# Weight differences of the seven-product pairs on GpSimd, and three more such pairs in the down projection

## The chip, the cores and the metric

The kernel runs on one core of a Trainium2 chip. The metric is the device time of one execution in microseconds (us). Three runs of the kernel before took 1316.18 to 1316.69 us, with a median of 1316.56 us.

A core has five engines that run their own instruction streams in order and wait for each other by semaphores. TensorE (PE in the profile) multiplies matrices and writes to PSUM. VectorE (DVE), ScalarE (ACT) and GpSimd (POOL) work elementwise. SyncE (SP) only issues the weight loads here. The profile lists PE's weight loads as PEld.

## The reference: what is computed

One layer of an encoder trunk on 256 positions with 2048 channels, everything in float32:

```python
h = rms_norm(x, norm_mix)
proj = h @ w_in                          # 2048 -> 9216: u, v | q, k, v | two gates
y_a = gmlp_branch(u, v, ...)             # gelu, layer norm, mixing over 128-position chunks
y_b = neighbourhood_attn(q, k, v, rpb)   # 16 heads, windows on a 4 x 64 grid
merged = sigmoid(g_a) * (y_a @ w_branch_a) + sigmoid(g_b) * (y_b @ w_branch_b)
x = x + merged @ w_out                   # 2048 -> 2048
h = rms_norm(x, norm_ffn)
up = conv3(h @ w_up)                     # 2048 -> 11008, width-3 conv over positions
x = x + (silu(gate) * val) @ w_down      # 5504 -> 2048
return rms_norm(x, norm_final)
```

Almost all of the work is in the weight matrices: w_in, w_branch, w_out, w_up and w_down.

## The kernel before, in words

**Pieces.** All weights are read as a single list of *pieces*, planned before the kernel starts: two row blocks of 128 by 512 columns, or two column blocks of 512 for one row block of 128 (a `plan_wide` piece). `load_to` issues the loads on SP into tiles `wraw`, of which there are `LOAD_AHEAD` (5). `split_to` splits each piece into a high part `whi` (ScalarE copies to float32r, line 151) and a low part `wlo` (VectorE subtracts the high part from the raw weights, line 152); there are four of each, and a piece is split up to three pieces ahead of its use. Activations are split in the same way, and a product is three matmuls: high by high, low activation by high weight, high activation by low weight. In the profile lines 291 to 293 are these three (`triple`).

**Order.** The order of every engine's instructions is the program's own order (`manual_schedule`). `begin(i)` opens piece i: it issues loads, issues the splits of the piece three ahead and then runs the tasks registered for it with `at(i, f)`. So a task at `i - 3` stands, on each engine, three pieces before the products of piece i.

**Wide groups and pairs.** A *wide* group multiplies 256 positions (two blocks t of 128) by 1024 columns (two blocks c of 512). The early projections of v and of the attention values, the second half of the two gates, the output projection (two groups) and the down projection (two groups of 43 pieces) are wide. A plain piece of a wide group is four products, one for each t and c: 12 matmuls. For some *pairs* of pieces, listed in `V_QUADS`, `VA_QUADS`, `GATE_QUADS`, `OUT_QUADS` and `DOWN_QUADS`, the group uses a scheme with seven block products for eight: the first piece of the pair takes three products, the second four. Entry q of such a list stands for the pieces 2q and 2q + 1 of its group.

**What a pair needs.** Sums of activation blocks (`act_sums`, `act_sums_split`, two to five pieces ahead, or made once for several groups) and differences of raw weight blocks:

- `weight_sums` at `i - 3` takes the two raw pieces (kept in `whole`) and makes four differences of 128x512 in two tiles `t13` and `t24`, each by one VectorE subtraction (lines 316 to 319).
- `weight_sums_split` at `i - 2` splits the two tiles into high and low parts `h13`, `l13`, `h24`, `l24`: two ScalarE copies (line 326) and two VectorE subtractions of 128x1024 (line 327).
- the first piece of a pair then needs only its first column block split, the second piece both (`units`).

The tiles of a pair exist once and take the memory of tiles that are idle at that stage (`first_room`, `sums_room`, `down_room`), so the profile shows them by those names: h, t, y, l. There are 29 pairs before: 2 and 3 in the early projections, 3 and 3 in the gates, 2 and 2 in the output projection, 7 and 7 in the down projection.

**GpSimd.** It has little to do: loads of the attention values and of the relative bias (lines 656 and 708), the selects that mask the bias (line 726), the residual x (line 927) and the last gain (line 1272). Its DMAs use descriptors that lie in a reserved part of SBUF.

Of the kernel before, what the change touches and what calls it, by code (L numbers as in the profile page):

```python
# [8 lines left out]
F32 = mybir.dt.float32  # L9
F32R = mybir.dt.float32r  # L10
AF = mybir.ActivationFunctionType
# [25 lines left out]
RMS_EPS = 1e-6  # L37
LN_EPS = 1e-5

LOAD_AHEAD = 5  # L40
SPLIT_AHEAD = 3
WAKE = (9, 8)
V_QUADS, V_ORDER = ((5, 6), (0, 1, 6, 7, 8, 9, 10, 11, 12, 13, 2, 3, 4, 5, 14, 15))
# [12 lines left out]
OUT_ORDER = (tuple(range(16)), (0, 1, 6, 7, 2, 3, 10, 11, 4, 5, 8, 9, 12, 13, 14, 15))  # L56
TURN_X2 = (13, 1)
Y_GAP = 224
DOWN_QUADS = ((4, 6, 9, 11, 14, 16, 18), (3, 5, 8, 10, 13, 15, 17))


@with_exitstack
def trunk_kernel(ctx, tc, x, norm_mix, w_in, ln_g, ln_b, w_s, b_s, rpb, w_branch, w_out,
                 norm_ffn, w_up, conv_k, conv_b, w_down, norm_final, out):
    nc = tc.nc
# [34 lines left out]
    def plan_wide(src, row0, order, c0):  # L100
        first = len(pieces)
        for k in order:
            pieces.append((src, row0 + k * 128, 2, (c0, 512, 1, 0), 512))
        return first
# [7 lines left out]
    def load_to(n):  # L112
        while n_loaded[0] < min(n, len(pieces)):
            i = n_loaded[0]
            n_loaded[0] += 1
            if i in preload:
                for f in preload[i]:
                    f()
            src, r0, kn, (c0, cn, nb, cs), step = pieces[i]
            w = wpool.tile([128, 2, 512], F32, name="wraw", bufs=LOAD_AHEAD)  # L120
            ld = src.shape[-1]
            if i == 0:
                for k in range(kn):
                    nc.sync.dma_start(w[:, k, :cn], src[r0:r0 + 128, c0 + k * step:c0 + k * step + cn])
            elif nb == 1:
                nc.sync.dma_start(
                    w[:, :kn, :cn],
                    bass.AP(tensor=src.tensor, offset=src.offset + r0 * ld + c0,
                            ap=[[ld, 128], [step, kn], [1, cn]]))
            else:  # L130
                for b in range(nb):
                    nc.sync.dma_start(
                        w[:, :kn, b * cn:(b + 1) * cn],
                        bass.AP(tensor=src.tensor, offset=src.offset + r0 * ld + c0 + b * cs,
                                ap=[[ld, 128], [step, kn], [1, cn]]))
            raw[i] = w
            if i in whole:
                whole[i] = w
# [30 lines left out]
    def at(i, f):  # L169
        tasks.setdefault(i, []).append(f)  # L170
# [6 lines left out]
    def begin(i):  # L177
        cur[0] = i
        load_to(i + LOAD_AHEAD)
        if i == 0:  # L180
# [83 lines left out]

    def wide(src, row0, order, c0, acts, quads, room, done, sums=None, odd=None):
        n0 = plan_wide(src, row0, order, c0)
        boxes = {}
        for n, q in enumerate(quads):  # L270
            i = n0 + 2 * q
            own = odd if odd and n % 2 else room
            whole[i] = whole[i + 1] = None
            units[i], units[i + 1] = 1, 2
            b = boxes[q] = {}
            if sums is None:
                b["acts"] = {}
                sum_acts_at(i - 5, i - 4, b["acts"], lambda k=order[2 * q]: ff["ap"][k // 2], room, "s")
            else:
                b["acts"] = sums[order[2 * q]]  # L280
            at(i - 3, lambda i=i, b=b: weight_sums(i, b, room))
            at(i - 2, lambda b=b, own=own: weight_sums_split(b, own))
        return ("wide", n0, order, acts, quads, boxes, done)

    def sum_acts_at(i, j, box, pair, room, name):
        at(i, lambda: act_sums(pair(), box, room))
        at(j, lambda: act_sums_split(box, room, name))
# [25 lines left out]
    def weight_sums(i, box, room):  # L313
        r0, r1 = whole.pop(i), whole.pop(i + 1)
        t13, t24 = room("t13", F32), room("t24", F32)
        nc.vector.tensor_sub(t13[:, 0], r0[:, 1], r0[:, 0])
        nc.vector.tensor_sub(t24[:, 0], r1[:, 1], t13[:, 0])
        nc.vector.tensor_sub(t13[:, 1], r1[:, 1], r0[:, 1])
        nc.vector.tensor_sub(t24[:, 1], r1[:, 0], t24[:, 0])
        box["w"] = (t13, t24)  # L320

    def weight_sums_split(box, room):
        u = []
        for name, t in zip(("13", "24"), box.pop("w")):
            h, l = room("h" + name, F32R), room("l" + name, F32R)
            nc.scalar.activation(h, t, AF.Copy)
            nc.vector.tensor_sub(l, t, h.bitcast(F32))
            u.append((h, l))
        box["t"] = {1: [x[:, 0] for x in u[0]], 3: [x[:, 1] for x in u[0]],
                    2: [x[:, 0] for x in u[1]], 4: [x[:, 1] for x in u[1]]}  # L330

    def run_wide(g, tail=0):
        kind, n0, order, acts, quads, boxes, done = g
# [176 lines left out]
    def first_room(name, dt):  # L510
        return ypool.tile([128, 2, 512], dt, name=f"y{first_rooms.index('t13' if name == 'f' else name)}")
# [387 lines left out]
    def ev_sums(j, room):  # L899
        def done(P, i):  # L900
            x2 = rs["x2"]
            p1, p5, p6, p7 = P
            x11, x12, x21, x22 = (x2[:, t, c * 512:(c + 1) * 512] for t in range(2) for c in (j, j + 1))
            m = {}

            def first_half():
                ab, cd = room("t13", F32), room("t24", F32)
                m["v"], m["u3"], m["w"] = cd[:, 0], cd[:, 1], ab[:, 0]
                nc.scalar.activation(ab[:, 0], p1, AF.Copy)
                nc.vector.tensor_add(x11, p1, x11)  # L910
                nc.vector.tensor_add(ab[:, 1], p6, ab[:, 0])
                nc.vector.tensor_add(m["v"], p5, ab[:, 1])
                nc.vector.tensor_add(m["u3"], p7, ab[:, 1])
                nc.vector.tensor_add(m["w"], p5, m["u3"])

            def second_half():
                nc.vector.tensor_add(x12, x12, m["v"])
                nc.vector.tensor_add(x21, x21, m["u3"])
                nc.vector.tensor_add(x22, x22, m["w"])

            at(i + 1, first_half)
            at(i + 2, second_half)
        return done
# [7 lines left out]
    def ev_out(g):  # L931
        def done(ps, i):
            x2 = rs["x2"]
            for t in range(NT):
                for c in range(2):
                    v = x2[:, t, (2 * g + c) * 512:(2 * g + c + 1) * 512]
                    nc.vector.tensor_add(v, ps[t][c], v)

            def squares(j):
                for t in range(NT):  # L940
                    nc.scalar.activation(junk, x2[:, t, j * 512:(j + 1) * 512], AF.Square,
                                         accum_out=rs["ss"][:, t, j:j + 1])

            for c in range(2):
                at(i + TURN_X2[g] + c, lambda j=2 * g + c: turn_x2(j))
                at(i + 3 + c, lambda j=2 * g + c: squares(j))
            if g == 1:
                at(i + 5, norm2)
        return done
# [7 lines left out]
    def turn_x2(j):  # L957
        x2 = rs["x2"]
        for k2 in range(2):
            p = bank()  # L960
            for kk in range(2):
                c = j * 4 + k2 * 2 + kk
                for t in range(NT):
                    nc.tensor.transpose(p[:, kk * T + t * 128:kk * T + (t + 1) * 128],
                                        x2[:, t, c * 128:(c + 1) * 128], ident)
            k = j * 4 + k2 * 2
            rs["h", k], rs["h", k + 1] = new_pair(hpool, f"h{k // 2}")
            split_pair(p, (rs["h", k], rs["h", k + 1]), gffn[:, k:k + 2])
# [128 lines left out]
    def odd_room(name, dt):  # L1097
        return s_room["odd"].tile([128, 2, 512], dt, name=name)

    first_sums = {2 * q: {} for q, _, _ in X_SUMS}  # L1100
    g_v = wide(w_in2, 0, V_ORDER, V0, xt, V_QUADS, first_room, (ev_v_sums, ev_v), first_sums,
               odd_room)
    g_va = wide(w_in2, 0, VA_ORDER, VA0, xt, VA_QUADS, first_room, (ev_va_sums, ev_va), first_sums)
    for n, (q, i, j) in enumerate(X_SUMS):
        sum_acts_at(i, j, first_sums[2 * q], lambda q=q: x_pairs[q],
                    lambda name, dt, i=i: first_room("s2" if name == "f" and i < 9 else name, dt), f"s{n}")
# [7 lines left out]
    def g_branch(br, j):  # L1114
# [5 lines left out]
    x_sums, m_sums = ({2 * q: {} for q in qs} for qs in (GATE_PAIRS, OUT_PAIRS))  # L1120
# [1 line left out]
                 (ev_gate_sums(br), ev_gate_wide(br)), x_sums) for br in range(2)]  # L1122
    g_m2 = [g_branch(br, j) for j in (2, 3) for br in range(2)]
    g_o = [wide(w_o, 0, OUT_ORDER[g], g * 1024, lambda k: mg["mT"][k], OUT_QUADS[g], sums_room,
                (ev_sums(2 * g, sums_room), ev_out(g)), m_sums) for g in range(2)]
    for n, q in enumerate(GATE_PAIRS):
        i = g_gw[0][1] - 3 + 3 * n
        sum_acts_at(i, i + 1, x_sums[2 * q], lambda q=q: x_pairs[q], sums_room, f"s{n}")
    for n, q in enumerate(OUT_PAIRS):
        i = g_o[0][1] + 3 + 3 * n  # L1130
# [7 lines left out]
    def down_room(name, dt):  # L1138
        return hpool.tile([128, 2, 512], dt, name=h_room[name])

    g_dn = [wide(w_d, 0, range(NF), g * 1024, lambda k: ff["a"][k], DOWN_QUADS[g], down_room,
                 (ev_sums(2 * g, down_room), ev_down if g == 0 else finish)) for g in range(2)]
# [166 lines left out]
```

## Time and profile before

| | before |
|---|---|
| runs (3), median | 1316.56 us |
| the profiled execution: span, first to last instruction | 1314.9 us |
| TensorE busy | 1303.3 us (99%), 6776 matmuls |
| VectorE busy | 1066.2 us (81%) |
| ScalarE busy | 764.8 us (58%) |
| GpSimd busy | 88.3 us (7%) |
| DMA, mean rate | 197 GB/s |
| granted TensorE clock, mean | 0.998 |

The span covers the first to the last instruction; the device time of a run holds a little more than it. A row of the profile's timeline gives the start and the length in us, the engine, the line, the operation, the tiles (out<-in), the shape, and the number of instructions put together; in square brackets stands the idle time of the engine just before, and what ended it. A row of the windows gives a stretch, its length, the busy time of PE, PEld, DVE, ACT and POOL, each with its instruction count, the granted clock, the DMA share and the rate. A row of the waits gives the waiting engine and line, what it waited for, the total, the count and the longest. A row for one line gives shortest/median/longest in ns.

### The profile page before, as it was taken

What the parts mean: (1) busy time and instruction counts of PE and PEld (TensorE: products, weight loads), DVE (VectorE), ACT (ScalarE), POOL (GpSimd) and SP (SyncE); (2) the same over time, 40 slices, a digit from 0 to 9 for tenths busy, and PEclk for the clock granted to TensorE, in tenths of its full rate; (3) what the DMA queues carried; (4) which work ended last, traced back from release to release, by engine and by line L of the source; (5) the groups of instructions that cost most, each with busy time, mean ns of one, the idle gap of its engine ahead of it and who ended that gap; (6) DMA issues with size and microseconds to landing.
All of it is one profiled execution on the core that took longest, in us unless ns stands there. A gap on an engine that the chain in (4) does not pass through costs nothing.

```text
span 1314.9 us, 19329 instructions
## 1 busy us (share of the span) xinstructions
PE 1303.3 (99%) x6776; PEld 1112.0 (85%) x6776; DVE 1066.2 (81%) x1625; ACT 764.8 (58%) x1139; POOL 88.3 (7%) x176
## 2 busy tenths in 40 slices
PE   9999999999999999999999999999999999999997
PEld 7888888888888888888888888888888888888885
DVE  7996778667789966986777778787878789999997
ACT  5766476666645644556555555555656556555653
POOL 0004505323000000000000000000000000000000
PEclk9999999999999999999999999999999999999999
DMA  8768656556556657665565665656565656666663
GB/s 305 260 209 235 201 174 201 181 163 194 179 172 209 210 190 241 204 210 163 175 202 182 192 193 182 195 184 193 180 205 177 198 154 226 220 194 206 210 202 119
DMA packets 170577, 259.37 MB, mean 197 GB/s; under 512 B 12664, under 2 KB 124144, under 8 KB 170480
## 3 DMA queue, kind: packets, MB, share of 16 engines
q1 hardware_dynamic: 166448, 250.31, 59.4%
q0 software_dynamic: 3712, 7.30, 2.4%
q8 instruction: 53, 0.87, 0.3%
q10 hardware_dynamic: 320, 0.53, 0.1%
q14 instruction: 44, 0.36, 0.1%
HBM read 253.90 MB, written 2.10 MB: 195 GB/s over the span
## 4 chain that ended last, share of the span: by engine, by line
PE 97%; DVE 1%; ACT 0%; issue 0%; DMA 0%; ACTq 0%; DVEq 0%
PE bank L205 31%; PE bank L209 16%; PE bank L293 12%; PE bank L291 12%; PE bank L292 12%; PE bank L233 5%; PE bank L235 4%; PE bank L234 4%; PE bank L761 1%; DVE wlo L152 0%; PE bank L811 0%; PE bank L503 0%; PE bank L627 0%; PE bank L801 0%; PE bank L892 0%
## 5 line engine op out<-in xcount | busy, mean ns | idle before, releaser
L152 DVE TENSOR_TENSOR wlo<-wraw,whi 128x1024 fp32r<-128x1024 f32 (+1 forms) x472 | 550.3, 1178 | 188.7 <-ACT whi L151 92.0
L151 ACT ACTIVATE whi<-wraw 128x1024 fp32r<-128x1024 f32 (+1 forms) x472 | 472.0, 1015 | 204.7 <-PE bank L292 75.2
L205 PE MATMUL bank<-h,whi 128*128 128x512 f32 x1760 | 426.0, 392 | 0.0
L205 PEld LDWEIGHTS bank<-h,whi 128*128 128x128 f32 x1760 | 321.9, 188 | 62.0 <-DVE ya L631 0.3
L209 PEld LDWEIGHTS bank<-h,wlo 128*128 128x128 f32 x1760 | 225.9, 191 | 8.8
L209 PE MATMUL bank<-h,wlo 128*128 128x256 f32 x1760 | 228.6, 283 | 0.0
L989 ACT ACTIVATE tc<-ta,ck 128x256 f32<-128x256 f32 x86 | 47.1, 594 | 117.1 <-DVE ta L987 117.1
L293 PE MATMUL bank<-wlo,a 128*128 128x512 f32 x260 | 101.5, 390 | 0.2 <-DVE wlo L152 0.2
L292 PE MATMUL bank<-whi,a 128*128 128x512 f32 x260 | 101.2, 389 | 0.0
L291 PE MATMUL bank<-whi,a 128*128 128x512 f32 x260 | 101.2, 389 | 0.0
L291 PE MATMUL bank<-whi,h 128*128 128x512 f32 x204 | 80.3, 393 | 0.0
L292 PE MATMUL bank<-whi,h 128*128 128x512 f32 x204 | 79.5, 390 | 0.0
L293 PE MATMUL bank<-wlo,h 128*128 128x512 f32 x204 | 79.5, 390 | 0.0
L293 PEld LDWEIGHTS bank<-wlo,a 128*128 128x128 f32 x260 | 48.8, 188 | 11.2 <-DVE wlo L152 1.3
L292 PEld LDWEIGHTS bank<-whi,a 128*128 128x128 f32 x260 | 48.8, 188 | 10.3
L291 PEld LDWEIGHTS bank<-whi,a 128*128 128x128 f32 x260 | 48.8, 188 | 10.1
L992 DVE SCALAR_TENSOR_TENSOR tc<-ta,ck,tc 128x255 f32<-128x255 f32 x86 | 41.4, 481 | 14.5 <-ACT tc L989 14.5
L979 ACT ACTIVATE tb<-bank 128x256 f32<-128x256 f32 x86 | 28.3, 385 | 42.2 <-PE bank L205 42.2
L233 PE MATMUL bank<-whi,y 128*128 128x512 f32 x128 | 50.5, 394 | 0.0
L233 PE MATMUL bank<-whi,h 128*128 128x512 f32 x128 | 50.4, 394 | 0.0
L235 PE MATMUL bank<-wlo,h 128*128 128x512 f32 x128 | 49.9, 390 | 0.0
L235 PE MATMUL bank<-wlo,y 128*128 128x512 f32 x128 | 49.9, 390 | 0.0
(299 smaller groups left out, 1744.1 us busy)
## 6 DMA issues: line engine op xcount, KB each, us to landing
wraw<-in_w_up_dram SPq DMA_DIRECT2D x336, 256.0 KB, 3.2
wraw<-in_w_in_dram SPq DMA_DIRECT2D x111, 512.0 KB, 4.5
wraw<-in_w_down_dram SPq DMA_DIRECT2D x86, 512.0 KB, 4.6
wraw<-in_w_in_dram SPq DMA_DIRECT2D x66, 256.0 KB, 3.2
wraw<-in_w_branch_dram SPq DMA_DIRECT2D x32, 512.0 KB, 4.5
wraw<-in_w_out_dram SPq DMA_DIRECT2D x32, 512.0 KB, 3.6
xs<-in_x_dram SPq DMA_DIRECT2D x8, 256.0 KB, 7.6
vw<-y POOLq DMA_DIRECT2D x16, 128.0 KB, 6.9
```

The lines of the kernel that those rows point to most:

```text
L151: nc.scalar.activation(h[:, k, :m], w[:, k, :m], AF.Copy)
L152: nc.vector.tensor_sub(l[:, k, :m], w[:, k, :m], h[:, k, :m].bitcast(F32))
L205: nc.tensor.matmul(p, h[:, k - k0, b * 128:(b + 1) * 128], acts(k), start=k == 0, stop=k == nk - 1)
L209: nc.tensor.matmul(p[:, :T], l[:, k - k0, b * 128:(b + 1) * 128], acts(k)[:, 0, :], start=False, stop=False)
L233: nc.tensor.matmul(p, xh, h[:, kk, :m], start=st, stop=False)
L234: nc.tensor.matmul(p, xl, h[:, kk, :m], start=False, stop=False)
L235: nc.tensor.matmul(p, xh, l[:, kk, :m], start=False, stop=sp)
L291: nc.tensor.matmul(p, xh, h, start=st, stop=False)
L292: nc.tensor.matmul(p, xl, h, start=False, stop=False)
L293: nc.tensor.matmul(p, xh, l, start=False, stop=sp)
L989: nc.scalar.activation(v, u, AF.Identity, scale=ck[:, 1, ch:ch + 1], bias=ck[:, 3, ch:ch + 1])
L992: nc.vector.scalar_tensor_tensor(v[:, 1:], u[:, :T - 1], ck[:, 0, ch:ch + 1], v[:, 1:], op0=OP.mult, op1=OP.add)
```

## The change

- `weight_sums` issues its four subtractions on GpSimd instead of VectorE, both halves of `t13` first, and stands five pieces ahead of the pair instead of three (three in the first group of the output projection, whose room opens late).
- `weight_sums_split` is cut in two: `t13` is split two pieces ahead, `t24` one piece ahead. The instructions are the same.
- `LOAD_AHEAD` goes from 5 to 7, and the reserved descriptor memory of GpSimd's DMAs goes to 4096 bytes of each partition, which leaves room for the two more raw tiles.
- `DOWN_QUADS` goes from 7 and 7 pairs to 9 and 8: every second pair of pieces, from pieces 4 and 5 on in the first group and from pieces 6 and 7 on in the second.

```diff
-LOAD_AHEAD = 5
+LOAD_AHEAD = 7
...
-DOWN_QUADS = ((4, 6, 9, 11, 14, 16, 18), (3, 5, 8, 10, 13, 15, 17))
+DOWN_QUADS = ((2, 4, 6, 8, 10, 12, 14, 16, 18), (3, 5, 7, 9, 11, 13, 15, 17))
...
-    def wide(src, row0, order, c0, acts, quads, room, done, sums=None, odd=None):
+    def wide(src, row0, order, c0, acts, quads, room, done, sums=None, odd=None, lead=5):
...
-            at(i - 3, lambda i=i, b=b: weight_sums(i, b, room))
-            at(i - 2, lambda b=b, own=own: weight_sums_split(b, own))
+            at(i - lead, lambda i=i, b=b: weight_sums(i, b, room))
+            at(i - 2, lambda b=b, own=own: weight_sums_split(b, own, 0))
+            at(i - 1, lambda b=b, own=own: weight_sums_split(b, own, 1))
...
-        nc.vector.tensor_sub(t13[:, 0], r0[:, 1], r0[:, 0])
-        nc.vector.tensor_sub(t24[:, 0], r1[:, 1], t13[:, 0])
-        nc.vector.tensor_sub(t13[:, 1], r1[:, 1], r0[:, 1])
-        nc.vector.tensor_sub(t24[:, 1], r1[:, 0], t24[:, 0])
+        nc.gpsimd.tensor_sub(t13[:, 0], r0[:, 1], r0[:, 0])
+        nc.gpsimd.tensor_sub(t13[:, 1], r1[:, 1], r0[:, 1])
+        nc.gpsimd.tensor_sub(t24[:, 0], r1[:, 1], t13[:, 0])
+        nc.gpsimd.tensor_sub(t24[:, 1], r1[:, 0], t24[:, 0])
         box["w"] = (t13, t24)
...
-    def weight_sums_split(box, room):
-        u = []
-        for name, t in zip(("13", "24"), box.pop("w")):
-            h, l = room("h" + name, F32R), room("l" + name, F32R)
-            nc.scalar.activation(h, t, AF.Copy)
-            nc.vector.tensor_sub(l, t, h.bitcast(F32))
-            u.append((h, l))
+    def weight_sums_split(box, room, n):
+        t = box["w"][n]
+        name = ("13", "24")[n]
+        h, l = room("h" + name, F32R), room("l" + name, F32R)
+        nc.scalar.activation(h, t, AF.Copy)
+        nc.vector.tensor_sub(l, t, h.bitcast(F32))
+        box["t"][1 + n] = (h[:, 0], l[:, 0])
+        box["t"][3 + n] = (h[:, 1], l[:, 1])
...
     g_o = [wide(w_o, 0, OUT_ORDER[g], g * 1024, lambda k: mg["mT"][k], OUT_QUADS[g], sums_room,
-                (ev_sums(2 * g, sums_room), ev_out(g)), m_sums) for g in range(2)]
+                (ev_sums(2 * g, sums_room), ev_out(g)), m_sums, lead=5 if g else 3) for g in range(2)]
...
-    nc = _bacc.Bacc("TRN2", target_bir_lowering=False, num_devices=1)
+    nc = _bacc.Bacc("TRN2", target_bir_lowering=False, num_devices=1, dynamic_dma_scratch_size=4096)
```

More of the change, by code (lines that the diff above doesn't have):

```diff
@@ L315, in weight_sums @@
         t13, t24 = room("t13", F32), room("t24", F32)
-        nc.vector.tensor_sub(t13[:, 0], r0[:, 1], r0[:, 0])
-        nc.vector.tensor_sub(t24[:, 0], r1[:, 1], t13[:, 0])
-        nc.vector.tensor_sub(t13[:, 1], r1[:, 1], r0[:, 1])
-        nc.vector.tensor_sub(t24[:, 1], r1[:, 0], t24[:, 0])
+        nc.gpsimd.tensor_sub(t13[:, 0], r0[:, 1], r0[:, 0])
+        nc.gpsimd.tensor_sub(t13[:, 1], r1[:, 1], r0[:, 1])
+        nc.gpsimd.tensor_sub(t24[:, 0], r1[:, 1], t13[:, 0])
+        nc.gpsimd.tensor_sub(t24[:, 1], r1[:, 0], t24[:, 0])
         box["w"] = (t13, t24)
-    def weight_sums_split(box, room):
-        u = []
-        for name, t in zip(("13", "24"), box.pop("w")):
-            h, l = room("h" + name, F32R), room("l" + name, F32R)
-            nc.scalar.activation(h, t, AF.Copy)
-            nc.vector.tensor_sub(l, t, h.bitcast(F32))
-            u.append((h, l))
-        box["t"] = {1: [x[:, 0] for x in u[0]], 3: [x[:, 1] for x in u[0]],
-                    2: [x[:, 0] for x in u[1]], 4: [x[:, 1] for x in u[1]]}
+        box["t"] = {}
+    def weight_sums_split(box, room, n):
[6 more added lines that the diff above has]
+        box["t"][3 + n] = (h[:, 1], l[:, 1])
     def run_wide(g, tail=0):
```

## The prediction

> **What bounds the kernel now.** I read four views in this order: the page, TensorE's waits, the windows by stage, and the rows where VectorE and GpSimd meet. Throughout, PE, DVE, ACT and POOL are TensorE, VectorE, ScalarE and GpSimd.
>
> ```profile
> span 1314.9 us, 19329 instructions
> PE 1303.3 (99%) x6776; PEld 1112.0 (85%) x6776; DVE 1066.2 (81%) x1625; ACT 764.8 (58%) x1139; POOL 88.3 (7%) x176
> PE 97%; DVE 1%; ACT 0%; issue 0%; DMA 0%; ACTq 0%; DVEq 0%
> PE bank L440 <- POOL ident masks.py:199: 1.4, 1, 1.4
> PE bank L291 <- ACT h L326: 0.6, 1, 0.6
> ```
>
> PE is busy 99% of the span, the chain that ended last is 97% PE, and the longest PE waits on anything are 1.4 us at the start and 0.6 us on one split of weight differences. So a faster helper engine can give PE almost nothing; time falls only if PE gets fewer matmuls. It rises as soon as a helper falls behind. How close are the helpers? These are the windows (length, then busy time of PE, PEld, DVE, ACT, POOL) of the stages that hold pairs with seven products: the two projections at the start, the wide gates, the output projection, and the two halves of the down projection.
>
> ```profile
> 20.00:90.00 70.00, 69.40 (x311) 57.14 (x310) 68.56 (x96) 48.77 (x71) 0.61 (x2) 1.00 0.74 245
> 384.00:470.00 86.00, 86.00 (x385) 71.32 (x384) 80.13 (x105) 49.16 (x56) 0.00 (x0) 1.00 0.61 200
> 530.00:585.00 55.00, 55.00 (x244) 45.54 (x243) 53.20 (x69) 30.37 (x39) 0.00 (x0) 1.00 0.62 207
> 1110.00:1200.00 90.00, 90.00 (x399) 74.53 (x398) 85.79 (x118) 48.62 (x55) 0.00 (x0) 1.00 0.64 211
> 1200.00:1290.00 90.00, 90.00 (x399) 74.53 (x398) 86.96 (x123) 53.60 (x67) 1.08 (x2) 1.00 0.61 201
> ```
>
> DVE is busy 93 to 98% there, POOL idle: DVE is a second bound right beneath PE, and taking work off it is worth something only if it then makes room for more pairs.
>
> **The change, part by part.**
>
> *Three more pairs.* The down projection has 14 pairs before and 17 after. A pair replaces eight products of three matmuls by seven.
>
> ```profile
> 38.84 0.39 PE L291 MATMUL bank<-whi,y 128*128 128x512 f32 x1
> 40.65 0.39 PE L293 MATMUL bank<-y,y 128*128 128x512 f32 x1
> 41.64 0.47 PE L291 MATMUL bank<-y,y 128*128 128x512 f32 x1 [0.60 <-ACT h L326]
> ```
>
> Between the first two rows lie eight starts in 1.81 us, 0.227 us for a matmul. Nine fewer matmuls take 2.0 us off PE. The third row starts 0.99 us after the one before it, so this one stall holds 0.76 us; with differences made earlier it can go. The most that the change can gain is therefore 2.0 + 0.76 = 2.8 us, 0.21%. (About 0.2%, 2.6 us, is what a measurement of this kernel can tell from no change.)
>
> *The differences leave DVE.* One pair and its two plain pieces, in the down projection:
>
> ```profile
> 1097.40 0.69 DVE L152 TENSOR_TENSOR wlo<-wraw,whi 128x512 fp32r<-128x512 f32 x1
> 1098.00 0.69 DVE L316 TENSOR_TENSOR h<-wraw 128x512 f32<-128x512 f32 x1
> 1100.54 1.22 DVE L152 TENSOR_TENSOR wlo<-wraw,whi 128x1024 fp32r<-128x1024 f32 x1
> 1101.68 2.35 DVE L327 TENSOR_TENSOR h<-h,h 128x1024 fp32r<-128x1024 f32 x2
> 1108.48 0.69 DVE L152 TENSOR_TENSOR wlo<-wraw,whi 128x512 fp32r<-128x512 f32 x1
> ```
>
> From the first row to its repetition for the next pair is 11.08 us of DVE work. PE needs (8 + 7) x 3 x 0.227 = 10.2 us for the same four pieces, which is why before spaces its pairs wider in places. The four subtractions run from 1098.00 to 1100.54: 2.54 us that leave DVE. What stays is 8.54 us, under 10.2. If POOL's work cost DVE nothing, a pair every four pieces would fit with 1.7 us to spare.
>
> *The differences arrive on POOL.* No row of before shows a subtraction on POOL. What it shows is POOL reading SBUF in one-input selects while DVE splits weights:
>
> ```profile
> 138.24 0.71 POOL L726 TENSOR_SCALAR_AFFINE_SELECT bias<-bias 64x512 f32<-64x512 f32 x1
> 138.61 1.41 DVE L152 TENSOR_TENSOR wlo<-wraw,whi 128x1024 fp32r<-128x1024 f32 x1 [0.60 <-DMA wraw<-in_w_in_dram]
> 208.67 2.46 DVE L152 TENSOR_TENSOR wlo<-wraw,whi 128x1024 fp32r<-128x1024 f32 x2 [0.26 <-issue]
> 208.80 2.50 POOL L726 TENSOR_SCALAR_AFFINE_SELECT bias<-run 64x128 f32<-64x128 f32 x2
> L726 POOL TENSOR_SCALAR_AFFINE_SELECT bias<-run x64: 298/312/1289, 131.7 to 309.9; 64x128 f32<-64x128 f32 x64
> ```
>
> The small select takes 0.30 us alone (the last row's smallest) and up to 1.29 us beside a split. The two engines take turns, whole instruction by whole instruction. At 138.61 the split is 0.19 us longer than its usual 1.22: it was let in at 138.80, 0.56 us after the select with 512 elements began. At 208.67 two splits take 2.46 us where two alike, back to back, take 2.35 (1101.68 above): one 128-element select slipped in between and cost DVE 0.11 us. Almost all of DVE's work in these stages has two inputs in SBUF, as the split has.
>
> Call c what one POOL subtraction (512 elements, two inputs) costs DVE. It reads eight times what the 128-element select reads: 8 x 0.11 = 0.88 us. Doubling the 512-element select's 0.56 gives 1.12. I take the middle, c = 1.0, an estimate. The ends: 0.44 if both inputs are read at once (4 x 0.11), and 1.42 if twice the select's whole 0.71 us is held. At c = 1.0 a pair takes 2.54 us off DVE and puts 4.0 us of blocking on it: 1.46 us worse.
>
> The Trainium skill, page "SBUF — State Buffer", section "Who interferes with whom", says that a DVE instruction with two SBUF inputs contends with a POOL instruction that reads SBUF, and that whoever starts second waits for all of the first. By that rule the rows above are the ordinary case, and the trace agrees (1.29 us against 0.30). Its page "GPSIMD Engine Reference", section 3.1, puts POOL's two-input rate at about 2.6 cycles of 1.2 GHz an element: 512 would be an estimated 1.11 us, and the sum below would end near 1370 us instead. No run here shows that rate yet.
>
> *The sum by stage* is DVE's deficit less the lead it holds, that is how long a piece's low part is ready before PE's first use of it. Pairs of rows: the end of a split, and the matmul that first reads it (x2 rows: their first split, 1.22 us).
>
> ```profile
> 84.60 2.35 DVE L152 TENSOR_TENSOR wlo<-wraw,whi 128x1024 fp32r<-128x1024 f32 x2
> 89.81 0.39 PE L293 MATMUL bank<-wlo,h 128*128 128x512 f32 x1
> 442.41 2.35 DVE L152 TENSOR_TENSOR wlo<-wraw,whi 128x1024 fp32r<-128x1024 f32 x2
> 447.22 0.39 PE L293 MATMUL bank<-wlo,h 128*128 128x512 f32 x1
> 562.63 2.35 DVE L152 TENSOR_TENSOR wlo<-wraw,whi 128x1024 fp32r<-128x1024 f32 x2
> 566.00 0.39 PE L293 MATMUL bank<-wlo,m 128*128 128x512 f32 x1
> 1092.53 1.22 DVE L152 TENSOR_TENSOR wlo<-wraw,whi 128x1024 fp32r<-128x1024 f32 x1
> 1097.28 0.39 PE L293 MATMUL bank<-wlo,a 128*128 128x512 f32 x1
> 1215.46 0.69 DVE L152 TENSOR_TENSOR wlo<-wraw,whi 128x512 fp32r<-128x512 f32 x1
> 1219.68 0.39 PE L293 MATMUL bank<-wlo,a 128*128 128x512 f32 x1
> ```
>
> Start: five pairs, 5 x 1.46 = 7.3, lead 89.81 - 85.82 = 4.0, stall 3.3 us. Gates: six pairs, 8.8, lead 3.6, stall 5.2. Output projection: three pairs by this point, 4.4, lead 2.15, stall 2.2. Down projection: a period is 8.54 + 4.0 = 12.54 us against PE's 10.2, so 2.34 us for each of 17 pairs, 39.8; leads 3.5 in the first half and 3.5 + 0.9 in the second (the row follows one pair, which cost 11.08 - 10.2); stall 39.8 - 7.9 = 31.9. Together 42.6, less the 2.8 gained: +39.8 us. The profiled execution has a span of 1314.9 us and the runs' median is 1316.56, 1.7 us more; the sum changes only the span, so it is added to the median: **1356 us**.
>
> *At nothing:* loads seven pieces ahead. SP waits for buffers, PE for no weight load:
>
> ```profile
> SPq L126 <- DVE wlo L152: 426.8, 200, 7.5
> L769 DVE SCALAR_TENSOR_TENSOR sc<-bank,bias x32: 407/422/429, 180.5 to 347.5; 64x256 f32<-64x256 f32 x32
> 141.22 0.51 POOL L726 TENSOR_SCALAR_AFFINE_SELECT bias<-bias 64x256 f32<-64x256 f32 x1
> ```
>
> The deeper queue serves POOL's earlier reads; without it the differences could not start five pieces ahead. The smaller descriptor space could make POOL's own DMA issues wait. Their first burst and the selects on it are done at 141.7 us, and the first reader comes at 180.5: 39 us hide it. If that cover went, the attention scores would wait by the excess; I take zero, and no reason for a gain. In the output projection the subtractions queue behind four loads of x on POOL, and in the down projection behind the gain loads, which wait for DVE; both have three or more pieces (over 8 us) before a split needs them.
>
> *Two splits, one piece apart:* the same two ACT copies and two DVE subtractions, the second pair of them a piece later. PE reads those halves in the pair's second piece, after two other products; the step is three pieces to two ahead, over 5 us, and I cost it at nothing. Each new pair also brings its sums of activations and its splits to DVE; they are inside the 11.08 us. In the first half the first pair now lies four pieces earlier, where the lead is the 3.5 us used above and not more, because DVE still finishes the up-projection's last group there.
>
> *The wait added:* ACT's and DVE's splits of the differences now wait for POOL, and behind ACT's stand the next weight splits, then PE. Four subtractions that each sit out one split (1.22) and hold 1.0 take 8.9 us, inside a 10.2 us period, so POOL itself is not late; the price is DVE's.
>
> **The rivals.** *The port costs little* (c of 0.6 or less, POOL reading both inputs together): at 0.56 the down projection's deficit is 0.58 x 17 = 9.9, 2 us over its lead, and the time is 1315.8, no change; below 0.5 nothing stalls and it is 1316.56 - 2.8 = 1313.8, just faster. For it: the low end of the select rows. Against: a second input must come from somewhere. *POOL holds longer* (c over 1.25): at 1.42 each period is 14.2 us, the down projection stalls 60, the earlier stages 34, and the time is 1408; from about 1.3 the POOL chain itself (4 x 2.5) fills the period. Against: the select's hold, 0.56, is well below its 0.71. *Half of it* (c of 0.62 to 0.7, idle DVE moments taking part of the holds): 1318 to 1325.
>
> **How the numbers follow.** The main case, c from 0.7 to 1.25, gives 1325 (17 x 1.14 - 7.9 - 2.8 = 8.7) to 1387 (56.8 - 7.9 = 48.9, earlier stages 24.7, less 2.8): chance 0.77, likeliest 1356. Longer holds 0.06; half of it 0.05; the port costs little 0.12, split between faster and no change. Slower: 0.77 + 0.06 + 0.05 = 0.88. The range is the main case's.
>
> **What would show it.** Right: the four subtractions on POOL last 1.3 to 2.5 us beside DVE's splits; splits of 128x1024 grow from 1.22 toward 2 us; DVE stays near full in the down projection though 2.54 us a pair left it; PE's waits name DVE's low parts, and the period of four pieces is about 12.5 us. Wrong: splits that stay at 1.22 us beside POOL, or a PE that is still 99% busy.

## The result, and the profile after

The changed kernel takes 1371.26 us (median of four runs, 1369.24 to 1371.49) against 1316.62 us: a ratio of 1.041, with a 95% interval of 1.0396 to 1.0426. It is slower by 54.6 us. The forecast was 1356 us, 1325 to 1387.

The page of the changed kernel, its span, busy times and chain, and then its list of TensorE's waits (all, how often, the longest):

```profile
span 1369.6 us, 19402 instructions
PE 1318.0 (96%) x6767; PEld 1111.2 (81%) x6767; DVE 1123.5 (82%) x1533; ACT 769.3 (56%) x1148; POOL 330.5 (24%) x304
PE 76%; DVE 17%; issue 3%; POOL 2%; ACT 1%; DMA 0%; DVEq 0%; ACTq 0%; POOLq 0%
PE bank L294 <- DVE wlo L152: 25.2, 18, 3.8
PE bank L294 <- DVE h L329: 9.2, 10, 2.9
PE bank L294 <- DVE l L329: 3.4, 5, 1.2
PE bank L294 <- DVE y L329: 2.1, 2, 1.5
```

PE has nine matmuls fewer, and now waits for VectorE's low parts: of weights (line 152) and of differences (line 329). These four waits add up to 39.9 us of the 54.7 by which the span grew. The rest appears as PE's busy time, 14.7 us more than before: about 4.6 of them come from a lower granted clock (last section), the others are not taken apart here. VectorE shed 92 instructions, and yet is busy for 57 us longer. So its instructions became longer. The timeline of the changed kernel over one pair of the down projection shows how (start, length, engine; the last row is that of line 317 as a whole):

```profile
1162.08 1.22 DVE L152 TENSOR_TENSOR wlo<-wraw,whi 128x1024 fp32r<-128x1024 f32 x1
1162.24 2.20 POOL L317 TENSOR_TENSOR h<-wraw 128x512 f32<-128x512 f32 x1 [5.16 <-DVE h L329]
1163.22 2.32 DVE L329 TENSOR_TENSOR h<-h,h 128x1024 fp32r<-128x1024 f32 x1
1164.41 2.27 POOL L318 TENSOR_TENSOR h<-wraw 128x512 f32<-128x512 f32 x1
1165.46 1.77 DVE L299 TENSOR_TENSOR h<-a 128x512 f32<-128x512 f32 x1
1166.64 1.74 POOL L319 TENSOR_TENSOR h<-wraw,h 128x512 f32<-128x512 f32 x1
1167.27 1.26 DVE L301 TENSOR_TENSOR h<-h 128x128 f32<-128x128 f32 x1
1168.45 0.28 DVE L302 TENSOR_TENSOR h<-h 128x128 f32<-128x128 f32 x1
1168.46 1.42 POOL L320 TENSOR_TENSOR h<-wraw,h 128x512 f32<-128x512 f32 x1
1168.66 1.38 DVE L303 TENSOR_TENSOR h<-h 128x128 f32<-128x128 f32 x1
L317 POOL TENSOR_TENSOR h<-wraw x17: 1294/2202/3935, 1091.6 to 1324.7; 128x512 f32<-128x512 f32 x17
```

Read the ends. The subtraction of line 317 starts while a split of VectorE reads SBUF, waits for it, and ends at 1164.44. The next split, which alone takes 1.22 us, starts at 1163.22 and takes 2.32: it waits 1.10 us. Then line 318 waits for that split, the 128x512 sum after it waits for line 318 (1.77 us instead of 0.68), and even sums of 128 elements (0.29 us before) take 1.26 and 1.38 us. Four subtractions on GpSimd lengthen four instructions of VectorE by 1.10, 1.09, 0.97 and 1.10 us. The last row gives the same from GpSimd's side: 1.29 us where nothing is in the way, 2.20 in the middle of the list. A waiting VectorE counts as busy, so a busy share of 82% here is no sign of useful work.

In the two halves of the down projection (windows of the changed kernel; from the first matmul of a half to that of the next, and to the first of the last piece; length, then busy time of PE, PEld, DVE, ACT, POOL, then the granted clock):

```profile
1091.60:1230.70 139.10, 118.74 (x490) 92.80 (x489) 136.31 (x142) 66.34 (x84) 68.58 (x40) 0.98 0.55 177
1230.70:1357.50 126.80, 113.84 (x481) 90.33 (x480) 119.47 (x130) 61.99 (x80) 55.68 (x33) 0.99 0.45 147
```

The same stretches of the kernel before:

```profile
1080.30:1192.70 112.40, 112.40 (x496) 92.83 (x495) 108.14 (x154) 63.42 (x78) 1.13 (x2) 1.00 0.67 218
1192.70:1302.90 110.20, 110.03 (x485) 90.53 (x484) 103.97 (x150) 61.15 (x77) 1.08 (x2) 1.00 0.55 180
```

There PE was busy throughout. Now VectorE is busy for 98% and 94% of them, and PE has holes.

### The profile page after: what moved, and what is told of

Same layout as the page of the kernel before. It is cut to its first block, busy times and chain, and to the rows that moved or that the text cites. A ratio compares the mean times of both kernels' runs of the same rounds, so it can differ in the third digit from the quotient of the medians.

```text
span 1369.6 us, 19402 instructions
## 1 busy us (share of the span) xinstructions
PE 1318.0 (96%) x6767; PEld 1111.2 (81%) x6767; DVE 1123.5 (82%) x1533; ACT 769.3 (56%) x1148; POOL 330.5 (24%) x304
## 4 chain that ended last, share of the span: by engine, by line
PE 76%; DVE 17%; issue 3%; POOL 2%; ACT 1%; DMA 0%; DVEq 0%; ACTq 0%; POOLq 0%
PE bank L205 29%; PE bank L209 15%; PE bank L294 6%; DVE wlo L152 5%; PE bank L292 5%; PE bank L293 5%; PE bank L233 4%; PE bank L235 4%; PE bank L234 4%; DVE h L329 3%; DVE h L299 1%; DVE h L303 1%; DVE h L301 1%; DVE l L329 1%; PE bank L762 1%
## 5 line engine op out<-in xcount | busy, mean ns | idle before, releaser
L152 DVE TENSOR_TENSOR wlo<-wraw,whi 128x1024 fp32r<-128x1024 f32 (+1 forms) x472 | 580.6, 1242 | 183.9 <-ACT whi L151 87.4
L317 POOL TENSOR_TENSOR h<-wraw 128x512 f32<-128x512 f32 x17 | 36.0, 2119 | 606.3 <-PE bank L205 510.8
L294 PE MATMUL bank<-wlo,a 128*128 128x512 f32 x242 | 98.1, 405 | 24.1 <-DVE wlo L152 24.1
L293 PE MATMUL bank<-whi,a 128*128 128x512 f32 x242 | 96.4, 398 | 0.0
L292 PE MATMUL bank<-whi,a 128*128 128x512 f32 x242 | 96.2, 398 | 0.0
L292 PE MATMUL bank<-whi,h 128*128 128x512 f32 x207 | 82.1, 396 | 0.4 <-DVE g L532 0.4
L294 PE MATMUL bank<-wlo,h 128*128 128x512 f32 x207 | 81.1, 392 | 1.1 <-DVE wlo L152 1.1
L293 PE MATMUL bank<-whi,h 128*128 128x512 f32 x207 | 81.0, 391 | 0.0
L310 ACT ACTIVATE h<-h 128x512 fp32r<-128x512 f32 x17 | 10.7, 631 | 104.9 <-DVE h L304 65.0
L727 POOL TENSOR_SCALAR_AFFINE_SELECT bias<-run 64x128 f32<-64x128 f32 x64 | 32.9, 547 | 111.5 <-DVE sc L770 110.9
L329 DVE TENSOR_TENSOR h<-h,h 128x1024 fp32r<-128x1024 f32 x34 | 55.6, 1634 | 0.0
L293 PEld LDWEIGHTS bank<-whi,a 128*128 128x128 f32 x242 | 46.4, 192 | 10.3
L292 PEld LDWEIGHTS bank<-whi,a 128*128 128x128 f32 x242 | 46.6, 193 | 9.6
```

The source lines that it names most:

```text
L152: nc.vector.tensor_sub(l[:, k, :m], w[:, k, :m], h[:, k, :m].bitcast(F32))
L292: nc.tensor.matmul(p, xh, h, start=st, stop=False)
L293: nc.tensor.matmul(p, xl, h, start=False, stop=False)
L294: nc.tensor.matmul(p, xh, l, start=False, stop=sp)
```

## The experiments

The theory: each subtraction on GpSimd keeps VectorE's two-input instructions off SBUF for as long as it reads, about 1.06 us by the period of a pair, more than the 0.64 us that VectorE needed for the subtraction itself. (The way to SBUF on which the two engines take turns is called the port here, as in the prediction; the traces show the turns alone.) Rivals: the added pairs, the deeper loads or the smaller descriptor memory, GpSimd's results being late, or GpSimd's writes.

**Loads alone.** The kernel before with `LOAD_AHEAD = 7` and the 4096 bytes of descriptor memory.

> The kernel before with loads seven ahead and the smaller descriptor memory, nothing else. Blocking theory: 1316.6 us within 1 us. Rival, that the deeper load queue or the smaller descriptor memory costs part of the 55 us: over 1319.

Measured: 1316.64 us against 1316.72, ratio 0.9999 (0.9990 to 1.0009). The deeper queue and the smaller memory cost nothing that these runs show.

**The engine alone.** The changed kernel with the subtractions back on VectorE; three pieces ahead, since at the two neighbouring pairs of the first projection an in-order VectorE would otherwise have to overwrite a tile that it itself reads only later.

```diff
-    def wide(src, row0, order, c0, acts, quads, room, done, sums=None, odd=None, lead=5):
+    def wide(src, row0, order, c0, acts, quads, room, done, sums=None, odd=None, lead=3):
...
-        nc.gpsimd.tensor_sub(t13[:, 0], r0[:, 1], r0[:, 0])
+        nc.vector.tensor_sub(t13[:, 0], r0[:, 1], r0[:, 0])
...
```

> Everything of the change but the engine: 9 and 8 pairs, loads seven ahead, the two splits one piece apart; the four subtractions are back on VectorE, three pieces ahead. Blocking theory (each GpSimd subtraction costs VectorE about 1.06 us, its own subtraction only 0.64): the period of a pair falls from 12.8 to about 11.1 us, still over PE's 10.2, so 17 x 0.88 = 15 us less leads of 4 to 8, less 2.0 us of matmuls: 1320 to 1328 us. Rival, that the added pairs and not GpSimd cost the time: within 10 us of the changed kernel's 1371.

Measured: 1332.83 us, ratio 1.0122 (1.0107 to 1.0137), 5 us over the forecast's upper end. So of the 54.6 us, GpSimd makes 38.4, and what is left of the change 16.1: the three pairs with the work that they give VectorE, since the deeper loads cost nothing (the splits one piece apart were not tried alone). All of the 16.1 us lie in the down projection, which begins at 1080.35 us here, at 1080.30 in the kernel before and at 1091.61 in the changed one: the 11.3 us of the earlier stages, whose pairs are the old ones, are GpSimd's alone. In the down projection the matmuls that open two pairs, four pieces apart, start 11.05 us from each other, close to the 11.08 us of VectorE's work in the prediction; in the changed kernel the same two pieces are 12.77 us apart. Rows of this kernel first, then of the changed one:

```profile
1140.43 0.39 PE L292 MATMUL bank<-whi,a 128*128 128x512 f32 x1
1151.48 0.39 PE L292 MATMUL bank<-whi,a 128*128 128x512 f32 x1
```

```profile
1161.18 0.39 PE L292 MATMUL bank<-whi,a 128*128 128x512 f32 x1
1173.95 0.39 PE L292 MATMUL bank<-whi,a 128*128 128x512 f32 x1
```

About 4.7 us, nearly the 5 over the forecast, lie at the start of the down projection:

```profile
1094.98 0.80 PE L292 MATMUL bank<-whi,a 128*128 128x512 f32 x1 [2.70 <-ACT whi L151]
```

There VectorE makes the first pair's differences (1089.91 to 1092.52) ahead of the last convolutions of the up-projection. ScalarE, in order, waits for those before it splits the next piece, and PE for ScalarE. After this hole the starts of ten matmuls lie 0.43 us apart instead of 0.227, 2.0 us more.

**The pairs alone.** The changed kernel with the old list of pairs.

```diff
-DOWN_QUADS = ((2, 4, 6, 8, 10, 12, 14, 16, 18), (3, 5, 7, 9, 11, 13, 15, 17))
+DOWN_QUADS = ((4, 6, 9, 11, 14, 16, 18), (3, 5, 8, 10, 13, 15, 17))
```

> The change with the old list of 7 and 7 pairs in the down projection, the differences still on GpSimd. Blocking theory: the stages before stay at +11 us, and each of the 14 pairs costs VectorE 1.7 us more than before, 24 us, of which its idle time and leads take some 8 to 10: 1340 to 1346 us. Rival, the added pairs: about 1328 us, the stages before alone.

Measured: 1347.63 us, ratio 1.0227 (1.0210 to 1.0244), just over the range. Without a single pair more, moving the differences costs 31 us. Both parts of the change lose, and each loses more where the other is present (31 and 38 us, 16 and 24).

**No reading on GpSimd.** Each subtraction becomes a memset of the same half tile; the differences are left out.

```diff
-        nc.gpsimd.tensor_sub(t13[:, 0], r0[:, 1], r0[:, 0])
+        nc.gpsimd.memset(t13[:, 0], 0.01)
...
```

> The changed kernel with each of the four subtractions replaced by a GpSimd memset of the same 128x512 half tile: the differences are left out, every later wait on GpSimd stays, but GpSimd reads nothing. Blocking of VectorE by GpSimd's reads: VectorE's splits stay at 1.22 us, PE is full, and the time is 1316.6 - 2.0 - 0.8 = 1313.8 us, 1313 to 1316. Rivals: if waiting for GpSimd's results or its writes cost the time, over 1340 us.

Measured: 1315.64 us against 1316.72, ratio 0.9992 (0.9983 to 1.0001). Every wait on GpSimd is still there, and so are its writes and the lead of five pieces, and the 55 us are gone. From this kernel's groups and TensorE's waits:

```profile
L317 POOL MEMSET h<- 128x512 f32 x17 | 9.0, 529 | 631.7 <-PE bank L209 509.2 <-DVE h L329 96.8 <-DVE x L920 20.0
PE bank L294 <- DVE wlo L152: 0.9, 1, 0.9
PE bank L294 <- DVE h L329: 0.7, 1, 0.7
```

A memset takes 0.53 us. Blocking by writes and waiting for GpSimd's order are out. (A memset is also over sooner than a subtraction; the next kernel parts reading from length.) The kernel also shows what could be had: 1.1 us for seventeen pairs with free differences, and the interval holds no change. The 2.8 us of the prediction were too many, because the two waits in the last rows, at the start of the down projection, stay.

**One input instead of two.** Each subtraction becomes a copy of one of its inputs; the differences are left out.

```diff
-        nc.gpsimd.tensor_sub(t13[:, 0], r0[:, 1], r0[:, 0])
+        nc.gpsimd.tensor_copy(t13[:, 0], r0[:, 1])
...
```

> The changed kernel with each of the four subtractions replaced by a GpSimd copy of one of its two inputs, so the differences are left out: GpSimd reads one input of 512 elements instead of two. The prediction's own rows put one input's cost to VectorE at 0.44 to 0.56 us: a period of 10.3 to 10.8 us, and 1315 to 1322 us. Rival, that a GpSimd instruction of this size blocks VectorE for the same time whatever it reads: 1371.

Measured: 1318.04 us, ratio 1.0012 (1.0002 to 1.0021), inside the forecast. The rows of this kernel show a copy that waits for a split, and the next split that waits for the copy:

```profile
1166.25 1.22 DVE L152 TENSOR_TENSOR wlo<-wraw,whi 128x1024 fp32r<-128x1024 f32 x1
1166.39 1.55 POOL L317 COPY h<-wraw 128x512 f32<-128x512 f32 x1 [5.34 <-DVE h L329]
1167.38 1.63 DVE L329 TENSOR_TENSOR h<-h,h 128x1024 fp32r<-128x1024 f32 x1
```

1.63 less 1.22 is 0.41 us for 512 elements read once. For the same elements read from two inputs the changed kernel's rows show about 1.06. So it is in the whole traces: in the changed kernel 106 VectorE instructions are 0.96 to 1.12 us longer than the shortest of their line and shape, 1.07 in the mean; in this one no instruction is, but 94 are longer by 0.28 to 0.47 us, 0.38 in the mean; in the memset kernel there are four of the latter. The copy, at its shortest 0.61 us, is hardly longer than the memset's 0.53, and beside the memsets the longest split of weights stays at 1.42 us, against 1.41 in the kernel before. So it is reading that costs, and here two inputs cost more than twice what one does.

**Half of the subtractions on GpSimd.** Those of `t13` on GpSimd, those of `t24` on VectorE.

```diff
+            at(i - 3, lambda b=b: weight_sums_2(b))
...
-        nc.gpsimd.tensor_sub(t24[:, 0], r1[:, 1], t13[:, 0])
-        nc.gpsimd.tensor_sub(t24[:, 1], r1[:, 0], t24[:, 0])
...
+        nc.vector.tensor_sub(t24[:, 0], r1[:, 1], t13[:, 0])
+        nc.vector.tensor_sub(t24[:, 1], r1[:, 0], t24[:, 0])
```

> The changed kernel with the two subtractions of t13 on GpSimd, five pieces ahead, and the two of t24 on VectorE, three ahead. Blocking theory, per instruction: 8.54 + 2 x 1.06 + 1.27 = 11.9 us a period, half way between 1332.8 (none on GpSimd) and 1371.3 (all four): 1350 to 1354 us. Rival, that GpSimd's chain of four being late sets the time: close to 1333.

Measured: 1351.42 us, ratio 1.0264 (1.0249 to 1.0279). None, two and four subtractions on GpSimd give 1332.8, 1351.4 and 1371.3 us: close to a straight line, 9.6 us for each of the four places. The matmul that opens a pair comes every 12.03 us:

```profile
1161.22 0.39 PE L293 MATMUL bank<-whi,a 128*128 128x512 f32 x1
1173.25 0.39 PE L293 MATMUL bank<-whi,a 128*128 128x512 f32 x1
```

With the prediction's 8.54 us of VectorE's other work, 8.54 + 1.27 + 2c = 12.03 gives c = 1.11 us, and the changed kernel's 8.54 + 4c = 12.77 gives 1.06.

**Without the first pair.** The changed kernel with 8 and 8 pairs.

```diff
-DOWN_QUADS = ((2, 4, 6, 8, 10, 12, 14, 16, 18), (3, 5, 7, 9, 11, 13, 15, 17))
+DOWN_QUADS = ((4, 6, 8, 10, 12, 14, 16, 18), (3, 5, 7, 9, 11, 13, 15, 17))
```

> The changed kernel without the first of the nine pairs in the down projection's first half (8 and 8 pairs). If that pair found the lead of 3.5 us that the prediction gave it, it cost the excess of one period, 2.3 us: about 1369. If it found VectorE without any lead, because the up-projection's last group is still on it, it cost its whole VectorE work, 4 x 1.06 + 2.2 + 2.3 - 0.5 = 8.2 us: about 1363.

Measured: 1364.41 us (1361.09 to 1365.69), ratio 1.0360 (1.0344 to 1.0376): 6.9 us less than with the pair. In the profiled executions the first half of the down projection shrinks from 139.1 to 130.6 us, by 8.5; its window in this kernel:

```profile
1094.40:1225.00 130.60, 116.01 (x493) 91.18 (x492) 127.87 (x134) 64.25 (x81) 62.17 (x36) 1.00 0.58 190
```

The granted clock is 1.00 in this half, and 0.98 in the changed kernel's, where it costs about 3.0 us (last section). So the pair's own waiting is about 5.5 of the 8.5 us: well over the excess of a period, 2.3, but not its whole VectorE work, 8.2. The changed kernel's rows at that place (VectorE's and GpSimd's, then TensorE's):

```profile
1091.59 1.29 POOL L317 TENSOR_TENSOR h<-wraw 128x512 f32<-128x512 f32 x1 [510.77 <-PE bank L205]
1091.73 1.44 DVE L993 SCALAR_TENSOR_TENSOR tc<-ta,ck,tc 128x255 f32<-128x255 f32 x1 [0.33 <-ACT tc L990]
1096.45 2.28 DVE L152 TENSOR_TENSOR wlo<-wraw,whi 128x1024 fp32r<-128x1024 f32 x1
```

```profile
1098.79 0.50 PE L294 MATMUL bank<-wlo,a 128*128 128x512 f32 x1 [3.83 <-DVE wlo L152]
```

GpSimd's first subtraction falls among the convolutions of the up-projection's last group. One of them takes 1.44 us instead of 0.48. With four such delays, the last on the split itself, the low part of the second piece is ready at 1098.73, and PE has stood for 3.83 us.

## Why the prediction was right, and where its sizes were off

- *What bounds the kernel.* Right: PE first, VectorE right beneath it. The loss appears as PE waiting for low parts, as forecast.
- *The mechanism.* Right in nearly all rows: the engines take turns by whole instructions, a split beside a subtraction grows from 1.22 to as much as 2.33 us, and 124 of the 128 subtractions last 1.27 to 2.33 us. The write-only, one-input and half-way kernels came out inside the ranges that follow from it. Four subtractions, each the first of its four, did not get their turn and last 3.42, 3.93, 3.93 and 6.21 us. In the longest case it starts beside a split at 412.56, and four more VectorE instructions pass it, none of them lengthened. Three rows of that place:

```profile
412.72 6.21 POOL L317 TENSOR_TENSOR t<-wraw 128x512 f32<-128x512 f32 x1 [5.17 <-DVE l L329]
413.69 1.22 DVE L329 TENSOR_TENSOR l<-t,h 128x1024 fp32r<-128x1024 f32 x1
421.31 1.23 DVE L329 TENSOR_TENSOR l<-t,h 128x1024 fp32r<-128x1024 f32 x1 [3.52 <-ACT h L328]
```

Why these four were passed over stays open.

- *c.* Forecast 1.0 us, the middle of 0.88 and 1.12; measured 1.06 and 1.11. Doubling the one-input select's 0.56 was the better of the two roads. The page "GPSIMD Engine Reference" of the Trainium skill, section 3.1, led to an estimate of 1.11 us and to a time near 1370: the trace agrees with the first. That the time agrees too, 1371, is partly luck: with 1.11 the prediction's sum gives 16 us for the stages before the down projection, where 11.3 were measured, and 20 for the first half of it, where 26.7 were. The plain copy (0.41 us for one input) is close to the 0.44 that the prediction took from the 128-element selects.
- *The sum by stage.* The span grew by 54.7 us, against a forecast of 39.8:

| stage | forecast, less the matmuls saved | measured |
|---|---|---|
| start | 3.3 - 0.8 = 2.5 us | 4.8 us |
| gates | 5.2 | 5.2 |
| output projection | 2.2 | 1.3 |
| down projection, first half | 9 x 2.34 - 3.5 - 1.4 = 16.2 | 26.7 |
| down projection, second half | 8 x 2.34 - 4.4 - 0.7 = 13.6 | 16.6 |

(Measured: how much longer each stage takes in the trace after, from its first matmul to that of the next.) The term that was mis-sized most is the lead of the first half, 3.5 us. It was read at the seventh piece (1092.53 and 1097.28), but the first pair's differences are taken while PE is still at the end of the up-projection, and there, at the second piece, the low part is ready only as PE needs it. The rows of the kernel before, a split that ends at 1083.48 and the matmul that first reads it:

```profile
1082.26 1.22 DVE L152 TENSOR_TENSOR wlo<-wraw,whi 128x1024 fp32r<-128x1024 f32 x1
1083.53 0.50 PE L293 MATMUL bank<-wlo,a 128*128 128x512 f32 x1
```

With no lead the pair costs more than the excess of a period, as the kernel without it shows. The larger c makes about 2 us of each half (9 x 0.23 and 8 x 0.23), and the granted clock, which the sum did not have, about 3.0 in the first and 1.6 in the second. For the second half that is enough (3.4 for the 3.0 us over the forecast); in the first it makes 8.6 of 10.5 us with the lead, and 1.9 stay without an account. The three earlier stages together are within 1.4 us of the forecast, but as a sum of errors of both signs.

- *The gain.* Forecast 2.8 us if the port were free; the memset kernel shows 1.1, not apart from zero. (And for "half of it" the prediction's own sum gives 1320 us at c = 0.62, not 1318; nothing rests on it.)
- *The cover of the deeper loads and the smaller descriptor memory.* Right, 1316.64 us. GpSimd's own lateness, forecast as hidden: right in the main, for PE's waits name a copy of the differences (line 328) for 0.4 us only. But VectorE stands twice for one, 3.52 us in the row above after the long subtraction and 2.28 us in the first stage.
- The rival that the port costs little falls with the measured c; the one that GpSimd holds longer than 1.25 us falls too.

## What to carry to other kernels

Before moving elementwise work from VectorE to an idle GpSimd, look in the trace for two rows that overlap, a GpSimd instruction that reads SBUF and a VectorE instruction with two SBUF inputs, and subtract their usual lengths: here each 128x512 subtraction on GpSimd took 1.06 us from VectorE to save it 0.64. In this kernel the idle GpSimd could not relieve a saturated VectorE, because the two take turns at reading SBUF, and VectorE's busy share does not show the waiting. A memset there cost nothing. And a lead is read where the moved work lands, not two stages on.

## What was not expected

After some of the new holes the granted TensorE clock fell. Windows of the changed kernel around the 3.83 us wait (the third figure from the end is the clock), and a matmul from it:

```profile
1094.00:1098.00 4.00, 0.95 (x5) 0.45 (x3) 3.96 (x3) 1.15 (x2) 3.57 (x3) 1.00 0.42 172
1098.00:1102.00 4.00, 3.21 (x10) 2.58 (x11) 3.93 (x9) 2.02 (x5) 0.00 (x0) 0.76 0.53 156
1102.00:1106.00 4.00, 4.00 (x15) 3.16 (x15) 3.87 (x8) 1.48 (x3) 0.00 (x0) 0.81 0.57 163
```

```profile
1101.74 0.63 PE L294 MATMUL bank<-wlo,a 128*128 128x512 f32 x1
```

For seven or eight matmuls the starts lie 0.43 us apart instead of 0.227. It happens three times in the down projection, after holes of 3.8, 2.2 and 2.2 us, about 4.6 us in all (23 matmuls at 0.2 us more each); two of the three, 3.0 us, lie in the first half. The length of the hole alone does not decide. This one, in the first half too, is followed by no fall:

```profile
1115.23 0.50 PE L294 MATMUL bank<-h,h 128*128 128x512 f32 x1 [2.88 <-DVE h L329]
1114.00:1118.00 4.00, 2.77 (x12) 2.32 (x13) 3.97 (x5) 0.00 (x0) 2.70 (x3) 1.00 0.33 125
```

And a like slow stretch stands near 84 us in the traces of the kernel without the first pair and of the one with the old pairs, after a hole of 1.48 us; the changed kernel has that hole too, without the slow stretch. What decides stays open. That these stretches make the wider spread of the slowed kernels' times is likely, not shown. So a hole in PE can cost more than its own length.
